# A two-layer hybrid attention trunk: four small edits to its first loads, its row norms and its last scale

## The chip, the cores and the metric

The kernel runs on one core of a Trainium2 chip. A core has a matrix engine (TensorE, PE in the profile; its weight loads are shown apart as PEld), a vector engine (VectorE, DVE), an activation engine (ScalarE, ACT), a general engine (GpSimd, POOL) and a synchronisation engine (SyncE, SP). Each runs its own instructions in the order in which the program gives them, and waits on semaphores for the others. DMA transfers are issued from a queue that belongs to an engine (SPq, ACTq, POOLq in the profile) and moved by 16 DMA engines. SBUF is the on-chip memory of 128 partitions, PSUM the memory that matmuls write, here eight banks of 128 x 512 float32.

The metric is device time in microseconds of one execution, as the median over several. A profiled execution has a time of its own, and a span from its first to its last instruction.

## The reference

Everything is float32. The sequence has 256 rows of width 1024, and so has a fixed memory. Two layers are run; then the rows are normalised once more.

```python
def rms_norm(x, g):
    xf = x.astype(jnp.float32)
    y = xf * lax.rsqrt(jnp.mean(xf * xf, axis=-1, keepdims=True) + NORM_EPS)
    return (y * g.astype(jnp.float32)).astype(x.dtype)

def reference(x, mem, norm_g, w_in, mem_norm_g, w_mem_kv, w_out, final_norm_g):
    for layer in range(DEPTH):
        h = rms_norm(x, norm_g[layer])
        proj = jnp.einsum('btd,dc->btc', h, w_in[layer])       # 1024 -> 3584
        sb_q, sb_k, sb_v, sb_g, mb_q, mb_k, mb_v, mb_g, mem_q, mem_g = jnp.split(proj, split_at, axis=-1)
        o_sb = merge_heads(stick_breaking_attention(...)) * jax.nn.silu(sb_g)      # 6 heads
        o_mb = merge_heads(moba_attention(rotary q, rotary k, v)) * jax.nn.silu(mb_g)  # 6 heads
        m = rms_norm(mem, mem_norm_g[layer])
        mk, mv = jnp.split(jnp.einsum('bmd,dc->bmc', m, w_mem_kv[layer]), 2, axis=-1)
        o_mem = merge_heads(memory_attention(mem_q, mk, mv)) * jax.nn.silu(mem_g)  # 4 heads
        mixed = jnp.concatenate([o_sb, o_mb, o_mem], axis=-1)  # width 1024
        x = x + jnp.einsum('btc,cd->btd', mixed, w_out[layer])
    return rms_norm(x, final_norm_g)
```

With 256 rows the block-sparse attention has one block, and so is causal attention within it.

## The kernel before

**Products in two halves.** Every float32 operand of a projection is split in two numbers of a shorter format (`fp32r` in the profile): `hi`, a cast, and `lo`, the rest. A product takes three matmuls: hi by hi, hi by lo, lo by hi. The weights come from HBM in chunks of 128 rows by 768 columns into five buffers `raw` (`dma_chunk`, L367, on SyncE's queue). `hi_task` (L383) casts a chunk on ScalarE or VectorE, `lo_task` (L392) subtracts on VectorE and then issues the next chunk. Eight buffers of each half stand ahead of TensorE.

**Activations.** For layer 0 the inputs x^T and mem^T come transposed from HBM into `uT`. `scale_hi` (L554) multiplies each block of 128 rows of x^T by the gain's column in `gc` on ScalarE and writes `Thi`; `scale_lo` (L560) makes `Tlo` on VectorE. Both need `gc`, and the columns of it are the gains of both norms and both layers. The factor 1/rms of each row is applied later, at the results, as `rcx` (column) and `rbx` (broadcast over partitions by a matmul against a tile of -1, `negone`); likewise `rcm` and `rbm` for mem. For layer 1, `norm_task` (L531) multiplies the rows by 1/rms and the gain (the buffer `w`), transposes with four matmuls against the identity `cst` (line L226 in the profile) and splits again into `Thi` and `Tlo`.

**Row norms.** A row tile is 128 of the 256 rows (t = 0, 1). `stat_block` (L484) squares a piece of the rows on ScalarE with a running sum per row (the sum is read out by an instruction of its own, ACTIVATION_READ_ACCUMULATOR) and adds it up on VectorE (L488), with the division by 1024 and the epsilon. `rstd` (L492) raises the sum to the power -1/2 on GpSimd (L494), against a column `expo` of -0.5. This is done for eight tiles: two of x at the start, two of mem, two of x after layer 0, two after layer 1.

**Order.** The program is written out by a planner, `Sched`: tasks are generators that ask for an engine, for buffers and for results of other tasks; at each step the task that can start earliest is taken (ties within a slack go to the lower priority number), and an estimated cost is added to that engine's clock (`act`, L229, charges 0.833 ns per element plus 93 ns, and 93 ns more for each operand per row or sum; the power on GpSimd is charged 1100 ns). The planner runs when the program is built. What it fixes is the order of the instructions on each engine; on the chip they wait for each other by semaphores. The tile library gives the DMAs of SyncE's and ScalarE's queues one of eight semaphores in turn, so each such DMA waits until the eighth one before it has landed.

**Start.** Before any task runs, L414 to L425 issue the first loads: the gain columns, weight chunks 0 and 1 (192 KB each, the two halves of the first 128 rows), 2, 3 and 4 (384 KB), and x^T in six pieces. Meanwhile TensorE runs seven matmuls on a zeroed tile `junk` (L862). `main` (L856) then takes the first projection (`sb_qk`, 144 matmuls over eight blocks k of x^T).

**End.** `resid_task` (L825) adds a piece of the last projection (columns 0 to 383, 384 to 767, 768 to 1023) to the rows `xs`, sums its squares, and in layer 1 `gain_task` (L838) multiplies the piece by the final gain. `out_task` (L844) then takes 1/rms, multiplies columns 0 to 511 on ScalarE and 512 to 1023 on VectorE and issues two stores per row tile on SyncE's queue.

Of the kernel before, what the change touches and what calls it, by code (L numbers as in the profile page):

```python
# [190 lines left out]
def hybrid_trunk(ctx: ExitStack, tc: tile.TileContext, x, mem, norm_g, w_in, w_mem_kv, w_out,  # L191
# [69 lines left out]
    def R(*eng, **kw):  # L261
        kw["eng"] = [e if isinstance(e, tuple) else (e, 0.0) for e in eng]
        return kw

    def sb(name, shape, dt=F32):
        return cpool.tile(shape, dt, name=name)
# [6 lines left out]
    masks = sb("masks", [128, 2, 128], BF)  # L273
    negT = sb("negT", [128, 128], FR)
    negone = sb("negone", [128, 128], FR)
    expo = sb("expo", [128, 1])
    junk = sb("junk", [128, 512], BF)
    gb = sb("gb", [128, D])
    uT = sb("uT", [128, KT, 256])
# [33 lines left out]
    def dma(dst, src, name=None, q=None, now=0.0):  # L313
        (q or nc.sync).dma_start(dst, src)
        n = _free(dst) * 4 * dst.shape[0]
        dma_t["t"] = max(dma_t["t"], now) + n / 340.0
        if name:
            S.ready[name] = dma_t["t"] + 2200.0
# [90 lines left out]
    def load_xT(k0, k1, q=None):  # L409
        dma(uT[:, k0:k1, :], xT_r[:, k0:k1, :], ("xT", k0), q)  # L410
        for k in range(k0 + 1, k1):
            S.ready["xT", k] = S.ready["xT", k0]

    dma(gc, gcols, "gc")  # L414
    load_xT(0, 1, nc.scalar)
    dma_chunk()
    load_xT(1, 2, nc.scalar)
    dma_chunk()
    dma_chunk()
    load_xT(2, 3)  # L420
    dma_chunk()
    load_xT(3, 4)
    dma_chunk()
    load_xT(4, 6)
    load_xT(6, 8)  # L425
# [4 lines left out]

    def setup():
        yield R("pool")
        nc.gpsimd.memset(expo, -0.5)
        nc.gpsimd.memset(negone.bitcast(F32), -1.0)
        S.op("pool", 2400.0)
        S.mark("setup0")
        yield R("pool", need=["cst", "msk"])
        m = S.res["w"].items[0][2][:, :256]
        nc.gpsimd.tensor_copy(identb, ident)
        nc.gpsimd.tensor_copy(masks, m.rearrange("p (m c) -> p m c", m=2))  # L440
        nc.gpsimd.tensor_scalar(negT, m[:, 128:256], -1.0, -1.0, op0=OP.is_ge, op1=OP.mult)
        S.op("pool", 2400.0)
        S.mark("setup")
# [37 lines left out]
        prog["done"] = max(prog["done"], max(e[1] for m in p.kmap.values() for e in m) + 1)  # L481


    def stat_block(src, sst, i):  # L484

        act(junk[:, :src.shape[-1]], src, AF.Square, accum_out=sst[:, i:i + 1])
        yield R("dve")
        nc.vector.tensor_scalar(sst[:, 4 + i:5 + i], sst[:, i:i + 1], 1.0 / D,  # L488
                                sst[:, 3 + i:4 + i] if i else EPS, op0=OP.mult, op1=OP.add)
        S.op("dve", 75.0)  # L490

    def rstd(sst, n, r):  # L492
        yield R("pool", need=["setup0"])
        nc.gpsimd.tensor_tensor(r, sst[:, 3 + n:4 + n], expo, op=OP.pow)  # L494
        S.op("pool", 1100.0)

    def row_stats(l, t, src, key, rc, rb):

        for i in range(2):
            yield R("act", need=[(key, t)])  # L500
            yield from stat_block(src[:, i * 512:(i + 1) * 512], ss[l, t], i)
        if key == "mem":
            if t == 0:
                dma(gb, mem_r[:, 1, :], ("mem", 1), now=S.cur.t)
            else:
                bcast_row(norm_g[1], ("gb", 0))
        yield from rstd(ss[l, t], 2, rc[:, t:t + 1])
        _, (rn,) = yield R("dve", need=["cst"], alloc=["rn"])
        dg = rn[0][:, :128]
        nc.vector.tensor_scalar(dg, ident, rc[:, t:t + 1], -1.0, op0=OP.mult, op1=OP.mult)  # L510
        S.op("dve", 200.0)
        _, (pt,) = yield R("pe", alloc=["bank"], need=["setup0"])
        mm(pt[:, :128], negone.bitcast(F32), dg, True, True)
# [311 lines left out]
    def resid_task(l, i, t, acc, w, H):  # L825
        xb = xs[:, t, i * 384:i * 384 + w]
        yield R("dve")
        tt(xb, acc[:, :w], xb, OP.add)
        S.free("bank", acc)
        yield R("act")  # L830
        yield from stat_block(xb, ss[l, t], i)
        S.mark(("res", l, i, t))
        if i == 2 and l == 0:
            S.spawn(norm_task(l, t, H, ("h", 1, t)), 1, S.cur.t)
        elif i == 2:
            S.spawn(out_task(t), 0, S.cur.t)

    def gain_task(i, t, w):  # L838
        xb = slice(i * 384, i * 384 + w)
        yield R("dve", need=[("gb", 1), ("res", 1, i, t)])  # L840
        tt(xs[:, t, xb], xs[:, t, xb], gb[:, xb], OP.mult)
        S.mark(("gain", i, t))

    def out_task(t):  # L844
        r = ss[1, t][:, 7:8]
        yield from rstd(ss[1, t], 3, r)
        for j, (s, q) in enumerate(((slice(0, 512), nc.sync), (slice(512, D), nc.sync))):
            yield R("act" if j == 0 else "dve", need=[("gain", i, t) for i in range(j, 2 + j)])
            if j == 0:
                act(xs[:, t, s], xs[:, t, s], AF.Copy, scale=r)  # L850
            else:
                ts(xs[:, t, s], xs[:, t, s], r)
            q.dma_start(out_r[:, t, s], xs[:, t, s])


    def main():  # L856
# [19 lines left out]
        for l in range(DEPTH):  # L876
# [107 lines left out]
            for i, k0, k1 in ((0, 0, 6), (1, 0, 6), (0, 6, 8), (1, 6, 8), (2, 0, 8)):  # L984
                p = pieces[f"wo{i}", l]
                w = p.width
                for t in range(2):
                    if k0 == 0:
                        accs[i, t] = yield from bank()
                    yield from nat_unit(p, X, t, accs[i, t][:, :w], xneed, k0, k1)  # L990
                    if k1 == KT:
                        S.spawn(resid_task(l, i, t, accs[i, t], w, hN), 0, S.cur.t)
                        if l == 1:
                            S.spawn(gain_task(i, t, w), 3 if i == 2 else 70, S.cur.t)
                    elif i == 0 and t == 1:
                        prog["done"] = p.loc(6, 0)[0]
                if k1 == KT:
                    finish(p)
# [58 lines left out]
```

## Time and profile before

| | us |
|---|---|
| time, median of 3 (lowest to highest) | 297.28 (297.07 to 298.67) |
| the profiled execution's own time | 297.42 |
| its span | 295.6 |
| PE busy in the span | 284.4 (96%) |
| DVE, ACT, POOL busy | 229.1, 154.0, 12.4 |
| first matmul on real data starts at | 5.06 |
| last matmul starts at | 288.90 |

The granted TensorE clock has a mean of 0.995. Rows of the timeline give the start and the duration in microseconds, the engine, the line, the operation, the written and the read tiles, the shape and a count; brackets give how long the engine was idle before and what ended that. Buffer numbers are left out, so `hi` stands for any of eight. A row with a count x4 joins four neighbours. In the view by stage each window has its length, then busy microseconds and instruction count of PE, PEld, DVE, ACT and POOL, the granted clock, the DMA engines' share and GB/s. A line of the waits says who waited for whom: the total, how often, the longest.

### The profile page before, as it was taken

What the parts mean: (1) busy time and instruction counts of PE and PEld (TensorE: products, weight loads), DVE (VectorE), ACT (ScalarE), POOL (GpSimd) and SP (SyncE); (2) the same over time, 40 slices, a digit from 0 to 9 for tenths busy, and PEclk for the clock granted to TensorE, in tenths of its full rate; (3) what the DMA queues carried; (4) which work ended last, traced back from release to release, by engine and by line L of the source; (5) the groups of instructions that cost most, each with busy time, mean ns of one, the idle gap of its engine ahead of it and who ended that gap; (6) DMA issues with size and microseconds to landing.
All of it is one profiled execution on the core that took longest, in us unless ns stands there. A gap on an engine that the chain in (4) does not pass through costs nothing.

```text
span 295.6 us, 5613 instructions
## 1 busy us (share of the span) xinstructions
PE 284.4 (96%) x2107; PEld 269.5 (91%) x2107; DVE 229.1 (78%) x506; ACT 154.0 (52%) x348; POOL 12.4 (4%) x19
## 2 busy tenths in 40 slices
PE   7999999999999999999999997999999999999991
PEld 4999999999999999899899996889999999998991
DVE  4969899997698799984998539774896686799462
ACT  4556879744565559432544114443444665695042
POOL 0311000300000000000120000000000000000001
PEclk9999999999999999999999999999999999999998
DMA  7997957477134873175757465160648136512003
GB/s 237 387 371 237 371 158 222 156 229 231 59 91 146 278 209 117 55 232 161 217 180 265 146 206 156 59 192 26 211 133 238 42 100 170 195 53 92 0 0 142
DMA packets 36795, 50.05 MB, mean 169 GB/s; under 512 B 2337, under 2 KB 34465, under 8 KB 36769
## 3 DMA queue, kind: packets, MB, share of 16 engines
q1 hardware_dynamic: 36192, 48.39, 51.8%
q0 software_dynamic: 288, 1.05, 1.0%
q8 instruction: 16, 0.26, 0.4%
q10 hardware_dynamic: 288, 0.26, 0.3%
q14 instruction: 11, 0.08, 0.1%
HBM read 48.64 MB, written 1.05 MB: 168 GB/s over the span
## 4 chain that ended last, share of the span: by engine, by line
PE 88%; DVE 5%; DMA 2%; issue 2%; ACT 1%; POOLq 0%; POOL 0%; SPq 0%; ACTq 0%
PE bank L221 84%; PE bank L226 4%; DMA raw<-in_w_in_dram 2%; DVE lo L243 2%; DVE hi L258 1%; DVE xs L243 1%; ACT junk L239 0%; DVE a L247 0%; ACT hi L237 0%; ACT xs L239 0%; POOLq L1053 0%; DVE ss L488 0%; DVE w L247 0%; POOL ss L494 0%; DVE Tlo L243 0%
## 5 line engine op out<-in xcount | busy, mean ns | idle before, releaser
L243 DVE TENSOR_TENSOR lo<-raw,hi 128x768 fp32r<-128x768 f32 (+2 forms) x111 | 99.9, 920 | 2.4 <-ACT hi L237 2.3
L221 PE MATMUL bank<-Thi,hi 128*128 128x256 f32 x288 | 83.8, 292 | 0.7 <-DVE hi L258 0.7
L221 PE MATMUL bank<-Tlo,hi 128*128 128x256 f32 x288 | 81.9, 286 | 0.0
L221 PE MATMUL bank<-Thi,lo 128*128 128x256 f32 x288 | 81.8, 286 | 0.0
L237 ACT CAST hi<-raw 128x768 fp32r<-128x768 f32 (+2 forms) x63 | 50.0, 810 | 28.2 <-PE bank L221 13.6
L221 PEld LDWEIGHTS bank<-Thi,hi 128*128 128x128 f32 x288 | 55.9, 195 | 2.9 <-issue 2.6
L221 PEld LDWEIGHTS bank<-Tlo,hi 128*128 128x128 f32 x288 | 55.9, 195 | 0.0
L221 PEld LDWEIGHTS bank<-Thi,lo 128*128 128x128 f32 x288 | 55.9, 195 | 0.0
L221 PE MATMUL bank<-hi,Thi 128*128 128x384 f32 (+1 forms) x160 | 53.9, 337 | 0.0
L221 PE MATMUL bank<-lo,Thi 128*128 128x384 f32 (+1 forms) x160 | 52.0, 325 | 0.0
L221 PE MATMUL bank<-hi,Tlo 128*128 128x384 f32 (+1 forms) x160 | 51.9, 325 | 0.0
L258 DVE CAST hi<-raw 128x768 fp32r<-128x768 f32 (+2 forms) x48 | 26.0, 547 | 22.5 <-PE bank L221 17.4
L221 PE MATMUL bank<-hi,mxhi 128*128 128x384 f32 (+1 forms) x96 | 30.8, 321 | 0.0
L221 PEld LDWEIGHTS bank<-hi,Thi 128*128 128x128 f32 x160 | 30.2, 189 | 0.5 <-issue 0.5
L221 PE MATMUL bank<-lo,mxhi 128*128 128x384 f32 (+1 forms) x96 | 30.5, 317 | 0.0
L221 PE MATMUL bank<-hi,mxlo 128*128 128x384 f32 (+1 forms) x96 | 30.4, 317 | 0.0
L221 PEld LDWEIGHTS bank<-hi,Tlo 128*128 128x128 f32 x160 | 30.2, 189 | 0.0
L221 PEld LDWEIGHTS bank<-lo,Thi 128*128 128x128 f32 x160 | 30.1, 188 | 0.0
L239 ACT ACTIVATE w<-bank,st 128x256 f32<-128x256 f32 (+1 forms) x40 | 17.3, 450 | 11.3 <-DVE st L672 7.4
L221 PEld LDWEIGHTS bank<-hi,mxhi 128*128 128x128 f32 x96 | 18.1, 189 | 0.8 <-issue 0.8
L221 PEld LDWEIGHTS bank<-hi,mxlo 128*128 128x128 f32 x96 | 18.1, 189 | 0.0
L221 PEld LDWEIGHTS bank<-lo,mxhi 128*128 128x128 f32 x96 | 18.1, 189 | 0.0
(114 smaller groups left out, 358.4 us busy)
## 6 DMA issues: line engine op xcount, KB each, us to landing
raw<-in_w_in_dram SPq DMA_DIRECT2D x71, 384.0 KB, 4.2
raw<-in_w_out_dram SPq DMA_DIRECT2D x20, 384.0 KB, 4.4
raw<-in_w_mem_kv_dram SPq DMA_DIRECT2D x8, 384.0 KB, 4.1
uT<-memT_dram SPq DMA_DIRECT2D x8, 256.0 KB, 5.5
xs<-in_x_dram SPq DMA_DIRECT2D x2, 512.0 KB, 6.8
gb<-in_mem_dram SPq DMA_DIRECT2D x2, 512.0 KB, 6.0
raw<-in_w_mem_kv_dram SPq DMA_DIRECT2D x4, 256.0 KB, 4.2
raw<-in_w_in_dram SPq DMA_DIRECT2D x4, 256.0 KB, 3.1
```

The lines of the kernel that those rows point to most:

```text
L221: nc.tensor.matmul(out, lhsT=lhsT, rhs=rhs, start=start, stop=stop, **kw)
L226: nc.tensor.transpose(out, in_, idt)
L237: nc.scalar.copy(out, in_)
L239: nc.scalar.activation(out, in_, func, **kw)
L243: nc.vector.tensor_tensor(out, a, b, op=op)
L258: nc.vector.tensor_copy(out, in_)
```

## The change

Four edits are made together.

1. The gain columns `gc` go from SyncE's queue to ScalarE's, ahead of the pieces of x^T there. Weight chunk 0 is then the first transfer on SyncE's queue. x^T's blocks 2 and 3 become one transfer on ScalarE's queue in place of two on SyncE's.
2. 1/rms is taken on ScalarE, as exp(-ln(s)/2), with two activations of one column: `Ln`, whose bias operand is the sum of the earlier pieces and whose input is the last piece's sum, and `Exp` with the scale -0.5. The division by 1024 moves into the square (scale 1/32). The last piece's addition on VectorE and the power on GpSimd fall away, and `expo` with them. The activation table that the program loads at its start has both functions.
3. The last scale is cut at column 384: ScalarE does 384 columns, VectorE 640. For the second row tile ScalarE's 384 columns are stored from ScalarE's own queue.
4. The gain's task is spawned by the residual's task when the sum of squares has been planned, in place of waiting for its mark.

```diff
-    dma(gc, gcols, "gc")
+    dma(gc, gcols, "gc", nc.scalar)
+    dma_chunk()
     load_xT(0, 1, nc.scalar)
     dma_chunk()
     load_xT(1, 2, nc.scalar)
     dma_chunk()
+    load_xT(2, 4, nc.scalar)
     dma_chunk()
-    load_xT(2, 3)
-    dma_chunk()
-    load_xT(3, 4)
     dma_chunk()
     load_xT(4, 6)
     load_xT(6, 8)
...
-    def stat_block(src, sst, i):
-        act(junk[:, :src.shape[-1]], src, AF.Square, accum_out=sst[:, i:i + 1])
-        yield R("dve")
-        nc.vector.tensor_scalar(sst[:, 4 + i:5 + i], sst[:, i:i + 1], 1.0 / D,
-                                sst[:, 3 + i:4 + i] if i else EPS, op0=OP.mult, op1=OP.add)
-        S.op("dve", 75.0)
+    def stat_block(src, sst, i, n):
+        act(junk[:, :src.shape[-1]], src, AF.Square, scale=1.0 / 32, accum_out=sst[:, i:i + 1])
+        if i < n - 1:
+            yield R("dve")
+            nc.vector.tensor_scalar(sst[:, 4 + i:5 + i], sst[:, i:i + 1], 1.0,
+                                    sst[:, 3 + i:4 + i] if i else EPS, op0=OP.mult, op1=OP.add)
+            S.op("dve", 75.0)
 
     def rstd(sst, n, r):
-        yield R("pool", need=["setup0"])
-        nc.gpsimd.tensor_tensor(r, sst[:, 3 + n:4 + n], expo, op=OP.pow)
-        S.op("pool", 1100.0)
+        yield R("act")
+        act(r, sst[:, n - 1:n], AF.Ln, bias=sst[:, 2 + n:3 + n])
+        yield R("act")
+        act(r, r, AF.Exp, scale=-0.5)
...
-        yield from stat_block(xb, ss[l, t], i)
+        yield from stat_block(xb, ss[l, t], i, 3)
         S.mark(("res", l, i, t))
+        if l == 1:
+            S.spawn(gain_task(i, t, w), 0 if i == 2 else 70, S.cur.t)
...
-        yield R("dve", need=[("gb", 1), ("res", 1, i, t)])
+        yield R("dve", need=[("gb", 1)])
...
-        for j, (s, q) in enumerate(((slice(0, 512), nc.sync), (slice(512, D), nc.sync))):
-            yield R("act" if j == 0 else "dve", need=[("gain", i, t) for i in range(j, 2 + j)])
+        for j, (s, q) in enumerate(((slice(0, 384), nc.scalar if t else nc.sync), (slice(384, D), nc.sync))):
+            yield R("act" if j == 0 else "dve", need=[("gain", i, t) for i in ((0,), (1, 2))[j]])
```

Because the planner's costs and requests change, the built program also has another order in places. On TensorE the matmuls are the same in number. In layer 0 the stick-breaking sums, the two broadcasts of 1/rms for mem and the rotary transposes stand up to some dozen matmuls earlier or later. At the boundary between the layers the first group of four transposes stands behind 3 matmuls of the next projection (before: 12), and the second and third group stand together behind 27 matmuls of it more (before: 21 and 24 behind the first). Some casts change place between ScalarE and VectorE. From the middle of layer 0 to its end, and in layer 1 up to the tail, the order is the same but for a few neighbours.

More of the change, by code (lines that the diff above doesn't have):

```diff
@@ L275, in hybrid_trunk @@
     negone = sb("negone", [128, 128], FR)
-    expo = sb("expo", [128, 1])
     junk = sb("junk", [128, 512], BF)
@@ L432, in setup @@
         yield R("pool")
-        nc.gpsimd.memset(expo, -0.5)
         nc.gpsimd.memset(negone.bitcast(F32), -1.0)
@@ L500, in row_stats @@
             yield R("act", need=[(key, t)])
-            yield from stat_block(src[:, i * 512:(i + 1) * 512], ss[l, t], i)
+            yield from stat_block(src[:, i * 512:(i + 1) * 512], ss[l, t], i, 2)
         if key == "mem":
@@ L992, in main @@
                         S.spawn(resid_task(l, i, t, accs[i, t], w, hN), 0, S.cur.t)
-                        if l == 1:
-                            S.spawn(gain_task(i, t, w), 3 if i == 2 else 70, S.cur.t)
                     elif i == 0 and t == 1:
```

## The prediction

> **What bounds the kernel now.** I read the page's first part, then the busy time by stage, then who TensorE (PE) waited for, then the timeline at the places where it waited. First the head of the page.
>
> ```profile
> span 295.6 us, 5613 instructions
> PE 284.4 (96%) x2107; PEld 269.5 (91%) x2107; DVE 229.1 (78%) x506; ACT 154.0 (52%) x348; POOL 12.4 (4%) x19
> ```
>
> PE is busy for 96% of the span, so time can be gained or lost only where it is not. Busy time by stage (window, its length, busy time of PE, PEld, DVE, ACT and POOL with instruction counts, clock, DMA share, GB/s):
>
> ```profile
> 5.06:9.60 4.54, 4.54 (x21) 4.54 (x22) 4.26 (x8) 2.64 (x6) 0.00 (x0) 1.00 1.02 359
> 20.00:56.00 36.00, 36.00 (x274) 34.74 (x273) 32.10 (x72) 30.04 (x60) 2.23 (x3) 1.00 0.75 240
> 143.00:150.80 7.80, 7.07 (x59) 6.67 (x57) 7.33 (x14) 2.74 (x7) 2.08 (x2) 1.00 0.79 248
> 177.70:185.00 7.30, 5.10 (x32) 4.53 (x31) 7.29 (x14) 2.99 (x7) 0.00 (x0) 1.00 0.56 165
> 289.20:292.00 2.80, 0.00 (x0) 0.00 (x0) 1.85 (x5) 1.23 (x3) 0.66 (x1) 1.00 0.50 187
> ```
>
> Between the first real matmul (5.06) and the last (289.2) PE is idle at two places: 0.7 us at the layer boundary and 2.2 us at 177.7 to 185. After 289.2 it has nothing left, and 6.4 us of tail follow. PE's waits name the causes:
>
> ```profile
> PE bank L221 <- DVE ah L258: 1.9, 1, 1.9
> PE bank L221 <- DVE hi L258: 0.7, 1, 0.7
> PE bank L226 <- DVE w L247: 0.6, 1, 0.6
> ```
>
> The 1.9 us (stick-breaking split in layer 1) sits behind DVE work whose order the change leaves alone; I keep it. The 0.7 us is the start, the 0.6 us the boundary's normalisation: both are touched, and so is the tail.
>
> **Part 1, the start: -0.2 us.** The timeline (start, duration, engine):
>
> ```profile
> 0.72 0.38 SPq L314 DMA_DIRECT2D gc<-gcols_dram  x1
> 0.75 0.87 ACTq L314 DMA_DIRECT2D uT<-xT_dram  x2
> 1.17 1.37 SPq L314 DMA_DIRECT2D raw<-in_w_in_dram  x3
> 1.18 3.17 PE L221 MATMUL bank<-junk 128*128 128x512 bf16 x7 [1.18 <-DVE junk L859]
> 3.05 0.51 ACT L239 ACTIVATE Thi<-uT,gc 128x256 fp32r<-128x256 f32 x1 [1.05 <-DMA uT<-xT_dram]
> 4.55 0.36 DVE L258 CAST hi<-raw 128x384 fp32r<-128x384 f32 x1 [3.43 <-DMA raw<-in_w_in_dram]
> 4.73 0.51 ACT L239 ACTIVATE Thi<-uT,gc 128x256 fp32r<-128x256 f32 x1 [1.17 <-DMA uT<-xT_dram]
> 5.06 0.55 PE L221 MATMUL bank<-Thi,hi 128*128 128x256 f32 x1 [0.71 <-DVE hi L258]
> ```
>
> The first matmul needs hi (raw0, landed 4.53) and Thi (gc and row block 0 of x^T, landed 3.03). Each queue issues one transfer per about 0.45 us. gc leaves SyncE's queue, so raw0 is issued at 0.72 in place of 1.17. On ScalarE's queue gc now goes ahead of x^T block 0, which moves from 0.75 to about 1.17; block 1 goes to 1.6, and blocks 2 and 3, one transfer instead of two later on SyncE's queue, to 2.05. All four are out before ACT's first activation, so they hold nothing up there. Now raw0 is first on its queue and x^T block 0 second. What a second place costs, the DMA rows by stage show:
>
> ```profile
> 1.75:2.50 0.75, 0.75 (x4) 0.22 (x2) 0.00 (x0) 0.25 (x1) 0.00 (x0) 1.00 1.00 224
> 2.50:3.10 0.60, 0.60 (x3) 0.23 (x2) 0.00 (x0) 0.05 (x1) 0.00 (x0) 1.00 0.56 100
> ```
>
> The first transfers (x^T block 0 and gc) move until 2.5; then comes a slack 0.6 us at 100 GB/s before the second ones flow. First place took 2.28 us from issue to landing (0.75 to 3.03), second place 3.36 us (raw0, 192 KB) and 3.53 us (x^T block 1, 128 KB, 1.18 to 4.71). Best case: each keeps its own latency, hi's data lands at 0.72 + 3.36 = 4.08 and the first matmul starts 0.45 us earlier. Worst: block 0 takes block 1's 3.53 us, lands at 4.70, Thi is done at 5.23 and the matmul starts at 5.37, 0.31 us later. In between: gc is 16 KB, so its queue is free sooner than when a 128 KB block went first, and it has 128 KB to bring where raw0 had 192 KB; I take a landing at 4.2, Thi done at 4.73, plus the 0.14 us that lay between hi's end and the matmul: 4.87, so -0.2. What is late next is Thi in place of hi; Tlo, moved on DVE behind lo0, then follows Thi directly and is there before the three matmuls that precede it end.
>
> The Trainium skill speaks against a larger gain: "DMA: Bandwidth & Descriptors", section "Issuing engines are not separate DMA queues", says that transfers from several engines share the same 16 DMA engines, and issuing from several saves only the issuing time. That limits the start to the 0.45 us above, and the sum to 0.25 us better than mine.
>
> **Part 2, 1/rms on ScalarE.** Per row tile the last DVE partial sum (L488) and GpSimd's power (L494) go; Ln and Exp of one column come, eight pairs in all. No trace row shows either on one column. Bounds:
>
> ```profile
> 15.12 0.63 ACT L239 ACTIVATE junk<-xs 128x512 bf16<-128x512 f32 x1 [3.37 <-DMA xs<-in_x_dram]
> 144.25 0.42 DVE L243 TENSOR_TENSOR xs<-bank,xs 128x256 f32<-128x256 f32 x1
> 144.76 0.42 ACT L239 ACTIVATE junk<-xs 128x256 bf16<-128x256 f32 x1 [1.89 <-DVE xs L243]
> 145.09 0.19 ACT L239 ACTIVATION_READ_ACCUMULATOR junk<-xs 128x1 f32 x1
> 145.27 0.28 PE L221 MATMUL bank<-Thi,hi 128*128 128x256 f32 x1
> 145.74 0.88 POOL L494 TENSOR_TENSOR ss<-ss,expo 128x1 f32<-128x1 f32 x1 [86.90 <-DVE ss L488]
> 146.59 0.28 PE L221 MATMUL bank<-Thi,lo 128*128 128x256 f32 x1
> 146.66 0.75 DVE L247 SCALAR_TENSOR_TENSOR w<-xs,ss,gb 128x512 f32<-128x512 f32 x1
> 147.47 0.66 PE L226 MATMUL bank<-cst,w 128*128 128x128 f32 x4 [0.60 <-DVE w L247]
> 148.50 0.95 DVE L243 TENSOR_TENSOR lo<-raw,hi 128x768 fp32r<-128x768 f32 x1
> 149.37 0.68 DVE L243 TENSOR_TENSOR Tlo<-bank,Thi 128x512 fp32r<-128x512 f32 x1
> 149.97 1.41 DVE L247 SCALAR_TENSOR_TENSOR w<-xs,ss,gb 128x512 f32<-128x512 f32 x2
> 291.27 0.72 ACT L239 ACTIVATE xs<-xs,ss 128x512 f32<-128x512 f32 x1 [1.02 <-POOL ss L494]
> ```
>
> Below, a one-column ACT step takes 0.19 us; above, the 256-column 0.42. From 512 to 256 columns ACT drops 0.21, so the intercept is 0.21; an operand per row adds 0.09 (0.72 against 0.63). I take Ln 0.30 (its bias is one) and Exp 0.21, and with three handovers of 0.03 it is 0.60 us in all, between 0.47 and 0.93. The Trainium skill ("ScalarE: Activation LUTs", section "What ACT_TABLE_LOAD costs") gives 0.28 and 0.19; the sum by it is 0.05 us better.
>
> *Boundary, +0.1.* From the squares' end (145.28) to w's start (146.66) were 1.38 us; now w can start at 145.88, and its transposes at about 146.7 instead of 147.47. But the plan also moves the transposes: behind 3 matmuls of the next projection, where they stood behind 12. PE reaches them at 145.63 and idles 1.05 us, where it idled 0.76 (from 146.71), the other 9 matmuls following later. The second and third groups stand together, 27 matmuls behind the first, so PE wants them at 150.4 and 150.8. DVE's new order up to them is w, residual add, lo, hi, lo, Tlo, w, w; on the rows' durations (neighbours overlap by about 0.08) the second w is there at 150.2, the third at 150.95, 0.2 us late. One switch between transposes and matmuls falls away. Carried to the end of the boundary PE is 0.1 us later than now. Ends: -0.3 (Ln and Exp at the lower bound, w of the second tile never late) and +0.5 (upper bound, twice).
>
> *Layer 0, +0.1.* Six of the eight pairs lie here or at the boundary, beside a PE that never waits (the 20 to 56 row); that PE is the cover. But the planner, given other durations, reorders PE, DVE and ACT from 15 to 70 us, and the margin is thin:
>
> ```profile
> 43.25 0.55 DVE L243 TENSOR_TENSOR al<-a,ah 128x384 fp32r<-128x384 f32 x1
> 44.24 0.34 PE L221 MATMUL bank<-al,negT 128*128 128x384 f32 x1
> ```
>
> al is ready 0.44 us before PE takes it. In the new order these sums come 3 matmuls (0.36 us) earlier; following DVE's new order with the durations above I find al ready in time there, and misses of 0.1 to 0.2 us at the broadcast of the second memory tile. Ends 0 and +0.8 (two such margins missed in full). Moving gc and x^T past SyncE's weights costs nothing later: DMAs wait for the eighth before them in both versions, and matmuls of block k reach Tlo and lo about 2 us after these are ready.
>
> **Part 3, the tail: -0.5 us.**
>
> ```profile
> 288.90 0.28 PE L221 MATMUL bank<-lo,mxhi 128*128 128x256 f32 x1
> 289.16 3.66 SPq L853 DMA_DIRECT2D out_dram<-xs  x4
> 290.06 0.19 ACT L239 ACTIVATION_READ_ACCUMULATOR junk<-xs 128x1 f32 x1
> 291.27 0.49 DVE L251 TENSOR_SCALAR xs<-xs,ss 128x512 f32<-128x512 f32 x1 [0.44 <-POOL ss L494]
> ```
>
> From 290.25 to 291.27 it is 1.02 us, now 0.60: -0.42. ACT's scaling drops from 512 to 384 columns, 0.72 - 128 x 0.00082 = 0.61; DVE's grows to 640, 0.49 x 640/512 = 0.61 at most. Both end 0.1 us sooner: -0.53. ScalarE issues the second tile's 384 columns itself, so SyncE's last issue is no longer second in line (0.42 us). That is worth little, since the last two transfers are bound by bytes, as DMA by stage shows:
>
> ```profile
> 292.80:294.30 1.50, 0.00 (x0) 0.00 (x0) 0.00 (x0) 0.00 (x0) 0.00 (x0) 0.55 0.93 350
> ```
>
> 512 KB at 350 GB/s take 1.5 us either way. Gains DVE made by dropping the partial sum are hidden. Ends: -1.1 (both issues count, lower ACT bound) and 0 (upper bound, and the larger 320 KB transfer ending last).
>
> **Sum.** -0.2 + 0.1 + 0.1 - 0.5 = -0.5 us. The profiled execution took 297.42 us around its span of 295.6, 0.14 above the median 297.28; so 296.9 by the one and 296.8 by the other. I forecast 296.8, no change that 0.5% (1.5 us, about what a measurement here can tell) would show.
>
> **Rivals.** (a) *PE's clock rises earlier.* Real matmuls come every 0.216 us at first (21 in 4.54 us), later every 0.12 (145.27 to 146.59, 11 steps). PE ran junk until 4.35 and then idled 0.71 us. If the start's best case comes (idle 0.26 us) and the fast pace therefore sets in up to 3.4 us sooner, some 16 matmuls save 0.09 us each, less what the hi and lo supply then withholds, say -0.9; with the start's -0.45 in place of -0.2: 295.6. For: nothing but that gap separates junk from work. Against: the best landing is needed. By the Trainium skill ("TensorE: Matmul & The Clock Gate", Part 1) the clock is released after a busy window of about 3.4 us that runs free of the kernel's start, so chance decides as much as the gap. Chance, with a tail near its lower end counted in: 0.28.
> (b) *Slower: PE's new order outruns the vectors.* PE is in order; each task moved ahead by 0.4 to 1.1 us (stick-breaking sums, memory broadcast, boundary transposes) blocks all projections behind it. If Ln and Exp take the upper 0.93 us and the layer-0 margins of 0.44 us are gone, PE loses 0.8 us there and 0.5 at the boundary, and with a start at +0.3 and a tail at 0 it ends at 297.28 + 1.6 = 298.9. It decides from about 0.5 us of extra lateness per task. For: the boundary already idles longer in the new order. Against: the planner (L229) charges Ln 0.19 and Exp 0.09, 0.23 us less than I take, half of that point. Chance 0.14.
> (c) *It does nothing*: landing is bound by bytes, Ln and Exp cost as much as the power did: 297.3. Chance 0.10; it counts as no change.
>
> My own case has 0.48. Faster by over 0.5%: 0.28; within: 0.58; slower: 0.14. The range is 295.4 to 298.4: it takes in (a) and the milder half of (b); the sum's own ends alone would reach from 295.3 to 299.0, which all parts reach only together.
>
> **What would show it.** First matmul at about 4.9, waiting for Thi and not hi; Ln near 0.30 and Exp near 0.21; PE idle before the first transposes about 1.0 us; no PE wait over 0.3 us between 15 and 137; the wait of 1.9 us unchanged; tail from last matmul to end 5.9 us. A first matmul after 5.2, a wait over 0.5 us in layer 0, or fast matmuls before 8 us would make it wrong.

## The result: 1.0% slower, and where the time went

The kernel after takes 300.04 us (median of 6, 299.23 to 301.93), the kernel before beside it 297.06 us. The ratio is 1.0103, with a 95% interval of 1.0065 to 1.0140: 3 us slower, where 296.8 us and no change had been forecast. The profiled execution is the longest of the six (301.93 us); its page begins:

```profile
span 300.1 us, 5607 instructions
...
PE 287.7 (96%) x2107; PEld 272.4 (91%) x2107; DVE 227.8 (76%) x497; ACT 156.3 (52%) x365; POOL 3.4 (1%) x10
```

Against the page of before (295.6 us, PE busy 284.4 us with the same 2107 matmuls) the span is 4.5 us longer, and PE is *busy* 3.3 us longer for the same work. So only part of the loss is waiting; the rest is matmuls that ran slower. PE's waits in the kernel after:

```profile
PE bank L221 <- DVE ah L258: 1.9, 1, 1.9
PE bank L221 <- DVE hi L258: 1.2, 1, 1.2
...
PE bank L226 <- DVE w L247: 0.9, 1, 0.9
PE bank L221 <- ACT Thi L239: 0.7, 1, 0.7
PE bank L221 <- DVE lo L243: 0.4, 1, 0.4
```

The 1.9 us, the 0.9 us (0.6 before) and the 0.7 us at the first matmul were expected. The 1.2 us for `hi` and the 0.4 us for `lo` are new, and both lie near 10 us. To see where the delay builds up, take the start of the n-th matmul (counted from 0, with the seven on the zeroed tile) in both traces and subtract:

| n-th matmul | its start after, us | after minus before, us | stage |
|---|---|---|---|
| 24 | 8.73 | -0.10 | block 0 of the first projection |
| 32 | 11.83 | +1.70 | block 1 |
| 56 | 16.19 | +3.18 | block 2 |
| 260 | 41.89 | +3.21 | layer 0 |
| 500 | 77.95 | +3.56 | layer 0 |
| 1340 | 183.86 | +3.57 | after the boundary |
| 1400 | 197.30 | +5.11 | after the 1.9 us wait of layer 1 |
| 2060 | 288.51 | +5.11 | near the last |
| end of the span | 300.1 | +4.5 | the tail gives back 0.6 |

Four places, then: 1.8 us near 10 us, another 1.5 us right behind it, 0.35 us in layer 0, and 1.5 us in layer 1, where the change does nothing.

**The first place.** The timeline at the start (start, duration, engine):

```profile
0.74 2.82 SPq L313 DMA_DIRECT2D raw<-in_w_in_dram  x5
0.77 0.39 ACTq L313 DMA_DIRECT2D gc<-gcols_dram  x1
...
1.19 1.42 ACTq L313 DMA_DIRECT2D uT<-xT_dram  x3
...
4.49 0.51 ACT L239 ACTIVATE Thi<-uT,gc 128x256 fp32r<-128x256 f32 x1 [2.47 <-DMA uT<-xT_dram]
...
5.05 1.01 PE L221 MATMUL bank<-Thi,hi 128*128 128x256 f32 x3 [0.69 <-ACT Thi L239]
...
8.59 0.51 ACT L239 ACTIVATE Thi<-uT,gc 128x256 fp32r<-128x256 f32 x1 [3.19 <-DMA uT<-xT_dram]
...
9.13 0.48 DVE L247 SCALAR_TENSOR_TENSOR Tlo<-uT,gc,Thi 128x256 fp32r<-128x256 f32 x1 [3.15 <-ACT Thi L239]
...
9.53 0.55 DVE L258 CAST hi<-raw 128x768 fp32r<-128x768 f32 x1
...
10.12 0.96 DVE L243 TENSOR_TENSOR lo<-raw,hi 128x768 fp32r<-128x768 f32 x1
...
10.23 0.35 PE L221 MATMUL bank<-Thi,hi 128*128 128x256 f32 x1 [1.23 <-DVE hi L258]
...
11.13 0.39 PE L221 MATMUL bank<-Thi,lo 128*128 128x256 f32 x1 [0.43 <-DVE lo L243]
```

Read it from the bottom. PE waits for `hi` and `lo` of chunk 2, but these do not wait for their chunk: on VectorE they stand behind `Tlo` of block 1, which waited 3.15 us for `Thi`, which waited 3.19 us for block 1 of x^T. It landed at 8.57; before, it landed at 4.71. Everything else in that chain is 0.5 to 1 us of work in line. SyncE's queue issued all five weight chunks, 1.5 MB, in its first 2.8 us, and block 1 was in flight from 1.67 to 8.57. The queues between 4 and 7 us (packets, MB, share of the 16 engines; q1 is SyncE's, q10 ScalarE's):

```profile
q1 hardware_dynamic: 230, 0.65, 65.4%
q10 hardware_dynamic: 217, 0.21, 24.5%
```

Both queues moved nearly the same number of packets, 230 and 217, but ScalarE's moved a third of the bytes of SyncE's: a row of a weight chunk is one packet of 3 KB (768 columns), a row of an x^T block one of 1 KB. In these 3 us x^T on ScalarE's queue gets about one byte in four. That is not the whole of it: an estimate from the same rate (0.21 MB in 3 us) would bring the 128 KB of block 1 by 6.2 us if the queue had carried nothing else since block 0 landed at 4.40. But blocks 2 and 3 were under way on it too, and what of the 217 packets was theirs the trace does not say; why block 1 lands as late as 8.57 stays open in that part. The median landing of blocks 0 and 1, first of before, then of after:

```profile
uT<-xT_dram ACTq DMA_DIRECT2D x2, 128.0 KB, 2.9
```

```profile
uT<-xT_dram ACTq DMA_DIRECT2D x2, 128.0 KB, 5.1
```

**The second and the fourth place.** Neither is a wait. The view by stage, cut where the granted clock (the column after POOL) changes:

```profile
8.56:11.97 3.41, 1.76 (x13) 1.38 (x12) 2.80 (x6) 2.61 (x6) 0.00 (x0) 1.00 0.94 330
11.97:15.38 3.41, 3.41 (x19) 3.41 (x18) 3.41 (x6) 1.18 (x3) 1.33 (x3) 0.50 0.98 339
186.05:189.46 3.41, 1.33 (x6) 0.90 (x7) 3.41 (x9) 0.81 (x2) 0.00 (x0) 1.00 0.94 311
189.46:192.87 3.41, 3.41 (x14) 3.41 (x13) 2.21 (x5) 1.97 (x5) 0.00 (x0) 0.50 0.09 30
```

Twice a stretch of 3.41 us in which PE was busy for only 1.76 and 1.33 us is followed by a stretch of the same length at half the clock, in which PE is busy throughout and does half the work. Each such halved window costs about 1.5 us. The first follows the new stall; the second follows the 1.9 us wait of layer 1, which is as long as in the profile of before, where the clock stayed at 1.00. There the wait (182.36 to 184.26) lay across a boundary between two windows: the clock's record of that trace begins at 9.63 us, and 51 windows of 3.413 us later, at 183.71, one of them ends, with PE busy for 2.06 us in the window before it and 2.57 us in the one behind it:

```profile
180.30:183.71 3.41, 2.06 (x12) 1.74 (x11) 3.41 (x7) 0.45 (x1) 0.00 (x0) 1.00 0.80 227
183.71:187.13 3.42, 2.57 (x14) 2.15 (x15) 2.98 (x8) 2.03 (x5) 0.00 (x0) 1.00 0.67 231
```

**The third place and the rest.** The 0.35 us of layer 0 is at the rotary transposes: between matmuls 264 and 600, twelve of them (`cst` with `rn`) take 1.33 us in place of 0.98, and nothing else differs by more than 0.15. Boundary and tail:

```profile
148.63 0.18 ACT L239 ACTIVATION_READ_ACCUMULATOR junk<-xs 128x1 f32 x1
...
148.85 0.53 ACT L239 ACTIVATE ss<-ss 128x1 f32<-128x1 f32 x2
...
149.41 0.75 DVE L247 SCALAR_TENSOR_TENSOR w<-xs,ss,gb 128x512 f32<-128x512 f32 x1 [0.33 <-ACT ss L239]
...
150.22 0.66 PE L226 MATMUL bank<-cst,w 128*128 128x128 f32 x4 [0.89 <-DVE w L247]
...
294.02 0.28 PE L221 MATMUL bank<-lo,mxhi 128*128 128x256 f32 x1
...
295.90 0.61 ACT L239 ACTIVATE xs<-xs,ss 128x384 f32<-128x384 f32 x1
295.90 0.55 DVE L251 TENSOR_SCALAR xs<-xs,ss 128x640 f32<-128x640 f32 x1
```

From the squares' end (148.81) to `w` (149.41) are 0.60 us, the figure of the sum. PE idles 0.89 us before the transposes, and the table shows no net loss at the boundary. From the last matmul's start to the end of the span are 6.1 us (294.02 to 300.1) where there were 6.7 (288.90 to 295.6). The two activations by shape, Ln and then Exp of the first norm (count, busy us, mean ns):

```profile
L239 ACT ACTIVATE rcx<-ss 128x1 f32<-128x1 f32 x2 | 0.6, 294 | 0.8 <-DVE ss L486 0.8
...
L239 ACT ACTIVATE rcx<-rcx 128x1 f32<-128x1 f32 x2 | 0.4, 200 | 0.0
```

### The profile page after: what moved, and what is told of

Its sections match the earlier page's. It is cut to its first block, busy times and chain, and to the rows that moved or that the text cites. A ratio compares the mean times of both kernels' runs of the same rounds, so it can differ in the third digit from the quotient of the medians.

```text
span 300.1 us, 5607 instructions
## 1 busy us (share of the span) xinstructions
PE 287.7 (96%) x2107; PEld 272.4 (91%) x2107; DVE 227.8 (76%) x497; ACT 156.3 (52%) x365; POOL 3.4 (1%) x10
## 3 DMA queue, kind: packets, MB, share of 16 engines
q0 software_dynamic: 288, 1.05, 1.3%
HBM read 48.64 MB, written 1.05 MB: 166 GB/s over the span
## 4 chain that ended last, share of the span: by engine, by line
PE 89%; DVE 5%; DMA 2%; ACT 1%; issue 1%; ACTq 0%
PE bank L221 85%; PE bank L226 4%; DMA uT<-xT_dram 2%; DVE lo L243 2%; DVE hi L258 1%; DVE xs L243 1%; ACT junk L239 0%; ACT ss L239 0%; DVE a L247 0%; ACT hi L237 0%; DVE w L247 0%; ACT xs L239 0%; DVE ah L258 0%; ACT Thi L239 0%; DVE Tlo L247 0%
```

## The experiments

Each execution is recorded with its span and its mean granted clock. (1 - clock) x span is the time that the halved clock took from it; I call it the clock's cost. It is 0.3 to 2.1 us even where nothing is lost, because the clock also falls in the tail, where PE has no work. So I count executions with 2.3 us or more as those that lost a window in which PE had work. The clock is on record with three decimals, so the cost comes in steps of 0.3 us, and six executions of the other kernels at 2.06 to 2.09 us could be counted either way; before has none between 1.5 and 2.3. In the kernel before these are 32 of 79 executions over the three groups of runs (8 of 27, 16 of 35, 8 of 17). The cost leaves out the start: the clock's record begins between 3.85 and 10.15 us in the 14 profiles, and until then the matmuls come at half pace (in before every 0.216 us until 9.63, every 0.12 us behind it), although the column shows 1.00. Medians of before differ between the groups (297.3, 297.64, 297.47), so each kernel is set beside the before of its own group; the ratios are not quotients of the medians and can differ from them by some tenths of a per cent.

**The start undone, and the start alone.** `old_start` is the kernel after with one piece put back, `start_only` is the kernel before with that piece of after:

```diff
-    dma(gc, gcols, "gc", nc.scalar)
-    dma_chunk()
+    dma(gc, gcols, "gc")
     load_xT(0, 1, nc.scalar)
     dma_chunk()
     load_xT(1, 2, nc.scalar)
     dma_chunk()
-    load_xT(2, 4, nc.scalar)
     dma_chunk()
+    load_xT(2, 3)
+    dma_chunk()
+    load_xT(3, 4)
     dma_chunk()
```

> The kernel after with the first loads of before put back (gc first on SyncE's queue, x^T blocks 2 and 3 there too); 1/rms on ScalarE, the cut of the last scale and the spawn of the gain stay. TensorE's order is that of after, to the instruction. Theory 'start' (x^T block 1 lands 3.9 us late behind the weights, and TensorE stalls and is slowed after it): the stall goes, the first matmul starts at 5.0 to 5.1, TensorE waits for nothing until the boundary, and what is left is layer 0 +0.4, boundary 0, tail -0.6: 296.9 us (296.4 to 297.4) against 297.06 before. Rival 'order' (the new order of the instructions and the two new activations cost the time): 299.5 us or more.

> The kernel before with the first loads of after, and nothing else of the change. Theory 'start': the whole loss is there and no gain at the tail: 297.06 + 3.1 = 300.2 us (299.5 to 300.8), with x^T block 1 landing after 8 us, a TensorE wait of 1 us or more near 9 us and a drop of the granted clock to half some 3 us after the wait begins. Rival 'order': 297.5 us or less.

Measured beside a before of 297.30 us: `start_only` 300.30 us (ratio 1.0070, 1.0041 to 1.0099): by the medians the whole loss, by the ratio 2.1 us of it, with 8 of 10 executions at a clock's cost of 2.3 us or more. Its median clock's cost is 3.0 us where before has 1.5, and its median span less that cost 295.3 us where before has 294.2: about 1 us of the loss is time without the clock's part, and some 1.5 us is the clock's. `old_start` 298.17 us (1.0019, 1.0002 to 1.0035): most of the loss is gone, but not all that was expected. Its median span less the clock's cost is that of before (294.3 against 294.2 us); what remained was 7 of 12 executions with a lost window where before had 8 of 27. In the profiled one the stall behind block 0 and the halved window near 12 us are absent, and layer 1 has lost one. (Its first matmul waited 1.48 us for `hi`, since chunk 0 landed at 5.31 where it landed at 4.53 in the profile of before: the same loads do not always land at the same time.) So the start is the cause, and the first theory lacked something about layer 1.

**Block 1 in one line with the weights.**

```diff
     dma_chunk()
-    load_xT(1, 2, nc.scalar)
+    load_xT(1, 2)
     dma_chunk()
```

> The kernel after with one transfer moved: x^T block 1 goes on SyncE's queue, right behind weight chunk 1 and ahead of chunk 2, and no longer on ScalarE's. The orders of TensorE, VectorE and the rest of all queues are those of after. Theory 'two queues share by packets' (a 1 KB row of x^T on ScalarE's queue takes its turn against a 3 KB row of weights on SyncE's): in the same line as the weights block 1 lands at about 5 us, TensorE's wait near 9 us goes, no drop of the clock, 296.9 us (296.3 to 297.6). Rival 'the bytes bound it' (the DMA engines are full, so block 1 lands after 8 us wherever it stands): 299.5 us or more.

298.39 us beside 297.30 (1.0017, 0.9993 to 1.0041), between the two expectations. Block 1 lands earlier, though not at about 5 us:

```profile
6.23 0.51 ACT L239 ACTIVATE Thi<-uT,gc 128x256 fp32r<-128x256 f32 x1 [0.44 <-DMA uT<-xT_dram]
...
9.14 0.38 PE L221 MATMUL bank<-Thi,lo 128*128 128x256 f32 x1 [0.43 <-DVE lo L243]
```

`Thi` of block 1 starts at 6.23. In the five profiles with the loads of after it starts at 8.59, 8.33, 7.40, 7.19 and 6.63; in the seven with the loads of before, at 4.56 to 5.51. The bytes are the same and only the place of one transfer has changed, which speaks against the bytes in total as the only cause; but it is one profile, and its 6.23 is only 0.4 us under the lowest of the five. The stall behind block 0 shrinks from 1.66 to 0.66 us (0.23 and 0.43). Block 0, however, is later here, and the first matmul starts at 5.44 after a wait of 1.08 us, where it started at 5.05 after 0.69. The median span less the clock's cost is 294.3 us, as before; again 7 of 12 executions lost a window.

**The stall filled.** Seven matmuls on the zeroed tile, whose result is not used, between blocks 0 and 1:

```diff
                     prog["done"] = p.loc(k, 640)[0] + 1
+                    if k == 0:
+                        _, (fill,) = yield R("pe", alloc=["bank"])
+                        for _ in range(7):
+                            nc.tensor.matmul(fill, lhsT=junk[:, :128], rhs=junk, start=True, stop=True)
+                        S.free("bank", fill)
```

> The kernel after with seven matmuls on the zeroed tile put between block 0 and block 1 of the first projection, where TensorE stood idle from 8.9 to 10.2 us; their result is not used. The late landing stays. Theory 'the stall also costs the clock' (idle time for which TensorE is set back to half speed for 3.4 us, some 1.4 us of time): with TensorE busy the drop goes and the time is 300.0 - 1.4 = 298.6 us (298.2 to 299.1), though block 1 still lands after 8 us. Rival 'the drop comes by itself' (its place is chance, or follows from load and not from idle time): 299.7 to 300.5 us.

This missed: 300.52 us beside 297.30 (1.0088, 1.0057 to 1.0120). All 6 executions lost a window. In the profiled one block 1 was there at 6.63, earlier than expected, TensorE stays busy behind block 0 and the clock stays at 1.00 near 12 us, as the theory had it; but the profile of `start_only` keeps it there too, with the stall, so this one alone shows little. What it lost:

```profile
181.44:184.85 3.42, 1.51 (x8) 1.06 (x7) 3.42 (x8) 0.00 (x0) 0.00 (x0) 1.00 0.93 285
184.85:188.27 3.42, 3.12 (x12) 3.00 (x12) 2.83 (x7) 2.45 (x5) 0.00 (x0) 0.50 0.40 129
188.27:191.68 3.41, 3.41 (x12) 3.41 (x11) 1.15 (x3) 0.48 (x1) 0.00 (x0) 0.50 0.00 0
```

It is layer 1, and it lost two windows: one at half the clock with PE busy for 3.12 of 3.42 us did not bring it back. The question was now why layer 1 loses its window so often once something at the start is late.

**The layer 1 wait filled.** Eight such matmuls where PE waits 1.9 us for `ah`; TensorE's order is the same otherwise. `before_calm` is before with it, `after_calm` after, `old_calm` is `old_start` with it, and `tail_calm` before with the tail's edits (the last norm's 1/rms on ScalarE, edits 3 and 4 as they stand in the change's diff) and nothing else of it. The matmuls' result is not used.

```diff
     def pair_sums(l, c):
+        if l == 1 and c == 0:
+            _, (fill,) = yield R("pe", need=[("sp", l, 2 * c), ("sp", l, 2 * c + 1)], alloc=["bank"])
+            for _ in range(8):
+                nc.tensor.matmul(fill, lhsT=junk[:, :128], rhs=junk, start=True, stop=True)
+            S.free("bank", fill)
```

```diff
     def out_task(t):
         r = ss[1, t][:, 7:8]
-        yield from rstd(ss[1, t], 3, r)
+        yield R("act")
+        act(r, ss[1, t][:, 2:3], AF.Ln, bias=ss[1, t][:, 5:6])
+        yield R("act")
+        act(r, r, AF.Exp, scale=-0.5)
```

> The kernel before with eight matmuls on the zeroed tile in the place in layer 1 where TensorE stands idle for 1.9 us (the wait for ah); their result is not used, the order is the same otherwise. Theory 'a window with half of it idle costs the clock' (in the traces the granted clock is halved for 3.41 us after a window of that length in which TensorE was busy for 1.3 to 1.8 us, and not after windows with 2.1 us or more): with the wait filled no execution loses clock in layer 1; those at 298 us and above vanish, and the median goes from 297.3 to 297.0 us (296.6 to 297.3). Rival 'the clock falls by itself': about 3 of 10 executions stay 1.5 us above the rest.

> The kernel after with the same eight matmuls in layer 1. Theory 'start plus clock': the late x^T block still costs the stall at the start and, in most executions, one halved window right after it, but not the halved window in layer 1: 298.9 us (298.3 to 299.5), 1.8 us above before_calm. If the two halved windows had nothing to do with the loss: 300.0 us as the kernel after.

> The kernel after with the first loads of before and the same eight matmuls in layer 1. Theory 'edits 2 to 4 are worth their own sum' (layer 0 +0.4, boundary 0, tail -0.6): 0.2 us under before_calm (0.5 under to 0.1 over), near 296.8 us, and the 0.9 us by which old_start stood over before is gone, since it came from halved windows in layer 1. Rival 'edits 2 to 4 lose time': 0.5 us or more above before_calm.

> The kernel before with the same eight matmuls and with the tail's edits alone: 1/rms by two activations only for the last norm, the last scale cut at 384, ScalarE's own queue for the last 384 columns, the gain spawned with the square. Start, layer 0 and boundary are those of before, and TensorE's order is that of before_calm to the instruction. Theory: the tail's 0.6 us without layer 0's 0.4: 0.6 us under before_calm (0.3 to 0.9), near 296.4 us. Rival 'the tail is bound by the bytes of the last stores': within 0.2 us of before_calm.

| | median us (12 executions) | ratio to before (297.64), 95% interval | lost a window |
|---|---|---|---|
| before_calm | 296.79 | 0.9967 (0.9946 to 0.9989) | 0 |
| old_calm | 296.91 | 0.9970 (0.9945 to 0.9996) | 0 |
| tail_calm | 296.32 | 0.9947 (0.9929 to 0.9966) | 0 |
| after_calm | 297.74 | 1.0011 (0.9986 to 1.0037) | 2 |

Two stretches of a window's length around that place in the profile of `before_calm` (the windows themselves lie 0.1 us later, with the same 2.95):

```profile
181.36:184.77 3.41, 2.95 (x15) 1.68 (x14) 3.28 (x9) 1.16 (x3) 0.00 (x0) 1.00 0.98 331
184.77:188.18 3.41, 3.41 (x22) 3.41 (x22) 2.42 (x6) 1.61 (x4) 0.00 (x0) 1.00 0.01 3
```

With PE busy for 2.95 us the next window keeps its clock, and no execution of the three kernels with the old start loses one by the count above. In layer 1 the wait is what costs the clock. The three differences: edits 2 to 4 together are worth nothing that can be told (296.91 against 296.79, expected 0.2 under); the tail alone is worth 0.47 us (expected 0.6, though the intervals of the two overlap); and `after_calm` stands 0.95 us over `before_calm`, where 1.8 us was expected, and only 2 of 12 executions lost a window. In its profile `Thi` of block 1 starts at 7.40 and the stall is 0.43 us; how long the stall is in the other executions is not on record. Beside the 3 us without the filling, about two thirds of the loss goes with the wait in layer 1: an estimate, since the two figures come from different groups.

**Why there?** A pure delay was added to the kernel before: eight or sixteen matmuls on the zeroed tile (1.7 or 3.4 us) ahead of the third projection piece, where PE never waits. The kernel after ran beside them again.

```diff
             for i, p in enumerate(ORDER[l]):
+                if l == 0 and i == 2:
+                    _, (fill,) = yield R("pe", alloc=["bank"])
+                    for _ in range(8):     # shift16: 16
+                        nc.tensor.matmul(fill, lhsT=junk[:, :128], rhs=junk, start=True, stop=True)
+                    S.free("bank", fill)
                 if l == 0 and i == MEM_AT:
                     mem_loads()
```

> The kernel after, unchanged, beside the next three. Theory 'the halved window in layer 1 comes more often when that stall lies later': 299.5 to 300.3 us, and in at least 8 of 10 executions the clock costs 2 us or more, where after_calm had 2 of 12. Rival 'it comes equally often, about 4 in 10': median 298.3 us, half of the executions near after_calm's 297.7.

> The kernel before with eight matmuls on the zeroed tile (1.7 us) put ahead of the third projection piece of layer 0, where TensorE never waits: everything after it, the 1.9 us stall of layer 1 too, comes 1.7 us later, and nothing else changes. Theory 'place against the clock's windows, which stand at nearly the same place in most executions': from the spread of the time that the clock cost in before_calm most windows end 2.0 to 2.8 us into their 3.41 us period from the span's start; 1.7 us later the stall lies wholly in one window in nearly all executions: 9 in 10 or more lose it, and the median is 297.4 + 1.7 + 1.5 = 300.6 us. Rival 'the windows stand anywhere': 4 in 10 lose it as in before, and the median is 299.1 us.

> The same with sixteen matmuls, 3.4 us, which is the length of one window. Theory 'place against the windows': the share of executions that lose the window in layer 1 is that of the kernel before again, 4 in 10, and the median is 297.4 + 3.4 = 300.8 us, hardly above shift, although twice as much was added. Rival 'the windows stand anywhere': 4 in 10 here too, but 1.7 us above shift.

| | median us | clock's cost, median us | lost a window |
|---|---|---|---|
| before, same group | 297.47 | 1.5 | 8 of 17 |
| shift (+1.7 us of work) | 300.45 | 3.0 | 6 of 6 |
| shift16 (+3.4 us of work) | 301.22 | 2.0 (three at 1.2 to 1.5, three at 2.4 to 3.0) | 3 of 6 |
| after_again | 300.61 (300.50 without the longest) | 3.3 | 10 of 12 |

1.7 us of harmless work cost 3.0 us, and the next 1.7 us only 0.8. `shift` came out as its theory had it; `shift16` and `after_again` are 0.3 to 0.4 us longer than theirs. In the profile of `shift` the wait lies wholly in one window:

```profile
182.09:185.50 3.41, 1.21 (x6) 0.64 (x5) 3.41 (x8) 0.19 (x1) 0.00 (x0) 1.00 0.88 256
185.50:188.92 3.42, 3.42 (x13) 3.26 (x13) 2.86 (x7) 2.14 (x5) 0.00 (x0) 0.50 0.28 103
```

Of the nine profiles with this wait unfilled, eight have 1.21 to 1.51 us of PE work in one window and lose the next; only before, with the wait across a boundary, has 2.06 and keeps it. So where the wait stands against the windows decides, and over the executions that place is not even: the kernel before loses the window in four of ten, with a delay of half a window six of six lose one, with a delay of a whole window three of six. With six executions each the shares are rough. For the kernel after this fits and is not shown one by one: its stall and layer 0 make it 1 to 2 us late by then, near the bad place, and 3.6 us late in the profiled execution, whose wait lies in one window but for 0.1 us. What ties the windows to the execution was not settled: the profiled executions, one of each kernel, show them at many places. One possible tie is in the traces but was not tested: TensorE runs at half pace until a window's end near the start, so how far the kernel has come depends on where the windows lie.

**A version that beats both.** `best` is `tail_calm` with chunk 0 first and gc second on SyncE's queue, x^T as before:

```diff
-    dma(gc, gcols, "gc")
-    load_xT(0, 1, nc.scalar)
     dma_chunk()
+    load_xT(0, 1, nc.scalar)
+    dma(gc, gcols, "gc")
     load_xT(1, 2, nc.scalar)
```

> tail_calm with one change at the start: weight chunk 0 goes first and gc second on SyncE's queue, x^T stays where it is in the kernel before. hi of chunk 0 needs only the chunk, Thi needs gc and x^T block 0 (landing at 3.0). If gc lands by 3.6 the first matmul follows the seven on the zeroed tile without a gap, at 4.4 in place of 5.06, and block 1 lands as before: 0.7 us under tail_calm, 295.6 us (295.0 to 296.0). Rival 'what PE gains at the first matmul it waits for at block 1 or 2, since the DMA engines are full': 296.3 us, as tail_calm.

296.04 us (median of 6, 295.44 to 296.40) beside a before of 297.47: ratio 0.9943 (0.9922 to 0.9964), and no execution lost a window. Over `tail_calm` (0.9947) the start adds nothing that can be told apart, and the profile shows what the rival named:

```profile
4.08 0.91 ACT L239 ACTIVATE Thi<-uT,gc 128x256 fp32r<-128x256 f32 x2 [2.08 <-DMA gc<-gcols_dram]
...
4.64 1.01 PE L221 MATMUL bank<-Thi,hi 128*128 128x256 f32 x3 [0.30 <-ACT Thi L239]
...
7.14 0.39 PE L221 MATMUL bank<-Thi,lo 128*128 128x256 f32 x1 [0.36 <-DVE lo L243]
```

gc lands just before 4.08, not by 3.6; the first matmul starts at 4.64 instead of 5.06, and 0.36 us of that is waited for at 7.14, for `lo` of chunk 1.

## Why the prediction was wrong, step by step

- **Start, forecast -0.2.** For the first matmul the step held roughly: it waits for `Thi` and not `hi`, block 0 landed at 4.40 (4.2 forecast, 4.70 at worst), and the matmul starts at 5.05 (4.87 forecast; 5.06 before). The step that failed is the one after it: "All four are out before ACT's first activation, so they hold nothing up there" and "Moving gc and x^T past SyncE's weights costs nothing later". Issue times were followed for every piece, but a landing time was worked out for block 0 alone. Block 1 went to third place on its queue, against five weight chunks in a row on the other; it landed 3.9 us later than before, and the supposed slack of 2 us between data and matmul was gone. The reason given, that each DMA waits for the eighth one before it in both versions, does not help: in the kernel after, x^T's last transfer waits for chunk 2 (landed at 7.92) and is issued at 7.93, where it was issued at 5.53. The step cost +1.8 us in the profile, and +1.5 us through the halved window that follows it in some executions; over the executions of `start_only` it is about 1 us without the clock's part.
- **The rule on queues.** The Trainium skill ("DMA: Bandwidth & Descriptors", section "Issuing engines are not separate DMA queues") has transfers from several engines share the same 16 DMA engines, and the rows between 4 and 7 us agree: the two queues' packets together take 90% of the engines' time. The prediction used it only as a limit to a gain. Turned round it speaks of a loss: what one queue is given earlier, the other gets later. The proportion, nearly packet for packet, is read from these rows alone.
- **"The wait of 1.9 us unchanged", kept at zero.** Its length is unchanged (1.9 us) and its price is not. The prediction used the granted clock only for the ramp at the start (rival a) and took 1.00 in the rows of one execution for granted everywhere else. In the kernel before four executions in ten already paid some 1.5 us there (with its first loads and the wait filled none of 36 did), in the kernel after 15 of 18 lost at least one window, there or at the start.
- **1/rms on ScalarE, 0.60 us.** Ln 0.294 (0.30 forecast), Exp 0.200 (0.21), the replacement 0.60 us to the hundredth. PE's idle time before the transposes is 0.89 us in the profile's brackets; the prediction counted from 0.12 us after the last matmul's start (0.76 where the bracket has 0.60), and so counted it is the 1.05 forecast. Boundary 0.0 (+0.1).
- **Layer 0, +0.1.** Measured +0.35 in the profile, inside its ends (0 to +0.8), but at the rotary transposes and not where it was worked out, at the broadcast of the second memory tile: that it lies inside the ends is luck; no single wait over 0.3 us, as forecast.
- **Tail, -0.5.** Measured -0.6 in the profile and -0.47 by `tail_calm`.
- **The rivals.** Rival (b), slower, gave 298.9 us, but its mechanism (PE's order outrunning the vectors in layer 0 and at the boundary) is worth 0.35 us. Rival (a) took the gap between the zeroed tile's matmuls and the first real one for what decides when the fast pace sets in; in the seven profiles with the loads of before the record begins at 3.99, 4.11, 4.60, 4.67, 9.28, 9.63 and 10.15 us, and 4.67 comes with a gap of 1.48 us, so the gap does not decide. None of the rivals had a late landing behind the first block, or a clock that falls again. The range could not hold 300 us without them. (The sum's ends, taken from its parts, are 295.4 and 298.9, not 295.3 and 299.0.)

## What to carry to other kernels

When loads are spread over queues, work out a landing time for *every* piece that the first matmuls need, not for the first: here two queues with work moved nearly the same number of packets, so the one with short rows brought a third of the bytes, and an engine that works in order passes one late block on to whatever stands behind it. Here a wait on TensorE of 1.9 us had a second price beside its length, and whether it was paid depended on where it fell; filled with eight matmuls on a zeroed tile, both the median and the scatter shrank (296.79 against 297.64 us). Before the effect of a small edit is read from medians that differ by less than 1%, look at the granted clock of each execution: `shift` and `shift16` differ by 1.7 us of work and by 0.8 us in time.

## What the runs showed of the hardware that was not expected

- In these traces the granted clock changes at the ends of windows of 3.413 us. At the start and in layer 1, PE busy for 1.2 to 1.8 us of one (1.21, 1.33, 1.51, 1.76) was followed by a window at half the clock; 2.06 us and more (before, 180.30 to 183.71: 2.06) was not. But busy time is not the measure: two windows in the tail with 1.62 us (`after_calm`, 288.46 to 291.88, and `bridge`, 290.67 to 294.08) kept the clock. Counted by the columns that the matmuls starting in a window stream (their second shape, 256 in 128x256), the windows at full clock of all 14 traces part, though by one matmul only: 2816 columns or fewer were followed by half the clock (after, 8.56 to 11.97: 11 matmuls of 256), 3072 or more were not (the two in the tail: 12 of 256). From half the clock, a window with 3.12 us busy did not bring it back (`bridge`), one busy throughout did; at the start, where the matmuls come at half pace, eight profiles have the full pace after a first busy window of 2.66 to 3.16 us, and in six a window of 2.31 to 2.84 us was not enough. The Trainium skill ("TensorE: Matmul & The Clock Gate", Part 1) has the length and calls the windows free-running, but speaks of a whole idle window; here some 1.7 us of idle time in one were enough in layer 1 and at the start.
- Free-running as the windows are called, their place against the kernel is not even over executions: with 1.7 us of added work 6 of 6 executions lost a window, with 3.4 us 3 of 6, with none 8 of 17 beside them (32 of 79 in all).
- Two queues that both had work moved 230 and 217 packets in 3 us, and 0.65 and 0.21 MB. The same first loads landed block 1 of x^T so that its `Thi` started at 6.63 in one execution and at 8.59 in another.
